# Three expert blocks joined on chip, the expert outputs read back ahead of the last weights, and the overflow loop moved into the middle of the stage

## The chip, the cores and the metric

One core of one Trainium2 chip. The metric is the device time of one execution in microseconds (us), taken as the median of the runs. Lower is better. PE is TensorE, DVE is VectorE, ACT is ScalarE, POOL is GpSimd and SP is SyncE; a "q" behind a name (SPq) is that engine's queue of transfers and waits.

## The reference, cut to what matters

Two layers. Each layer is a token mixer (gMLP in layer 0, RWKV-7 in layer 1) followed by a mixture of 32 experts; a final RMSNorm ends it. There are 768 tokens in layer 0 (512 latent and 256 context), and 512 in layer 1; a token is 1024 floats. All is float32. The part that the change touches is the experts' sum:

```python
def hier_moe(h, w_grp, b_grp, w_exp, b_exp, w_gate, w_up, w_down):   # h: n_tok x 1024
    ...                                   # router: two experts of 32 per token, with weights
    def expert_block(args):               # one block of up to 128 rows, one expert
        xb, e = args
        return (jax.nn.silu(xb @ w_gate[e]) * (xb @ w_up[e])) @ w_down[e]
    out = lax.map(expert_block, (buf.reshape(n_blocks, MOE_BLOCK, d), block_expert)).reshape(cap, d)
    y = jnp.zeros((n_assign, d), h.dtype).at[order].set(out[dest]).reshape(n_tok, TOP_K, d)
    return jnp.einsum('tk,tkd->td', weights, y)     # then x = x + gate * this
...
    return rmsnorm(x, final_g)                      # after the last layer, latent rows only
```

One expert has 1024x512 gate weights, as many up weights and 512x1024 down weights: 2 MB each, 6 MB in all. Every expert is used, so 192 MB of weights are read in each layer.

## The kernel before, in words

The experts are worked off in `Moe.experts`, in an order written once per layer (`self.seq`). A position of this order is one *unit*. A big unit (B) is one expert with up to 128 rows; a pair unit (p) is two experts with up to 64 rows each, which share the matrix engine by halves of its columns. Layer 0 has 12 p and 8 B, layer 1 has 13 p and 6 B. In the order of before, a p comes first, then B and p are mixed evenly, and a p is last. Positions are counted from 0: `gu(9)` below is the gate and up product of position 9.

A unit has these steps, in this order on PE: `gu` (L880: gate and up into the PSUM tile `gu_ps`, which needs the unit's gate and up weights), the hidden rows (ACT L943, DVE L944: `h_e`), their transposes (`eT_ps`, then `hT`), and `o` (L897: the down product into `o_ps`). The program places `o` of position i-1 after `gu` of position i. DVE scales `o_ps` to `yo` (L900), and POOL scatters `yo` by an indirect DMA (L809) into `ybuf`, a DRAM table with two rows per token. Rows of a unit's tokens come by a gather (`xg<-hbuf,idx`, POOL, L798).

The weights come in pieces of 1 MB, 12 pieces for a p, 6 for a B, issued by SP alone (`load`, L483, called by `fetch`). Pieces lie in the tiles `e_raw`: 13 buffers in layer 0, 15 in layer 1, handed out in rotation over three pools (`RAW = (2, 8, 3), (4, 6, 5)`: in layer 0 pieces go two to the first pool, eight to the second, three to the third, and again). A piece is issued when a buffer of its pool is free, which is when the product that read it is done, and when the eighth transfer before it has landed (SP's transfers have eight counters in turn). `want(i + 1)` makes the fetch of a unit stand one unit ahead of its `gu`; what SP does is in program order.

The last unit of a layer isn't scattered. Its `yo` is split in two parts (`y_parts`, L66 and L67) and each tile of 128 tokens takes its rows through a one-hot product (`c_ps`, L921) that DVE adds to the residual `x_res` (L924; `k.x` in the code). `early()` issues, when the last scatter is on its way, the reads of `ybuf` (L853: six pieces of 1 MB in layer 0, four in layer 1, into `e_raw`); POOL adds the two rows of each token (L856), DVE adds that to `x_res` (L916), for every third tile PE does it through the identity (L923). Then come, for each group of tiles, the squares (ACT L2093), a reciprocal root of few small instructions (L83 to L90), and in layer 0 the store of the tiles (`xd<-x_res`, SP), in layer 1 the final scaling (L2124, into `yo`) and the store of the output (L2125).

A unit may overflow in principle: `overflow` is a loop over a number `n_ov` that the chip works out. With this input it is zero and the loop's body never runs. It stands at the end of each layer's stage:

```python
        nv = nc.values_load(self.n_ov[:, 0:1], min_val=0, max_val=nmax)
        with tc.For_i(0, nv) as i:
```

The lines of the trace are those of the file before. The next stage after layer 0 begins with loads by SP (`a<-rw_a` L1313, `w_raw<-rw_wk` L1258), a memset by POOL (`hsel`, L1318), and DVE's scaling of `x_res` (L152).

Of the kernel before, what the change touches and what calls it, by code (L numbers as in the profile page):

```python
# [9 lines left out]
F32 = mybir.dt.float32  # L10
# [7 lines left out]
P = 128  # L18
# [305 lines left out]
class Moe:  # L324


    def __init__(self, k, l, n):
        self.k, self.l, self.n = k, l, n


        self.big = BIGS[l]
        self.pairs = (NE - self.big) // 2
        self.units = self.big + self.pairs

        self.nb = self.units + (2 * n * P) // 65
        rest, small = range(self.big), range(self.big, self.units - 1)
        self.seq = [self.units - 1] + [u for _, u in sorted(
            [((i + 0.5) / len(rest), u) for i, u in enumerate(rest)] + [((i + 0.6) / len(small), u) for i, u in enumerate(small)])]
        self.raw, self.slots = {}, 0
        self.scattered = []  # L340
# [14 lines left out]
    def open(self, ps, tag):  # L355
# [13 lines left out]
        self.tok = new([n], "tok")  # L369
# [132 lines left out]
    def route(self, rp, ps, after):  # L502
# [183 lines left out]
        u = self.seq[-1]  # L686
        for t in range(n):
            ts(self.tok[:, t:t + 1], tab[:, 1, u:u + 1], float(BIG - t * P), None, op0=ALU.add)
# [137 lines left out]
    def experts(self, ep, ps, after):  # L826
# [21 lines left out]
        def early():  # L848

            ys = []  # L850
            for t in range(n):
                y = self.slot().rearrange("p (k d) -> p k d", k=2)
                nc.sync.dma_start(y, self.ybuf[2 * t * P:2 * (t + 1) * P, :].rearrange("(p k) d -> p k d", k=2))  # L853
                ys.append(y)
            for y in ys:
                nc.gpsimd.tensor_tensor(y[:, 0, :], y[:, 0, :], y[:, 1, :], op=ALU.add)  # L856
            return ys

        xg, xT, hT = {}, {}, {}
# [4 lines left out]
        for i in range(N + 1):  # L864
# [5 lines left out]
            if i < N:  # L870
                want(i + 1)
                if i + XG - 1 < N:
                    xg[i + XG - 1] = self.gather(seq[i + XG - 1])
                q = {}
                for gu in range(2):
                    q[gu] = ps.tile([P, 512], F32, name="gu_ps", tag="gu", bufs=2)
                    for kk in range(KD):
                        f = slice(kk % 4 * 512, kk % 4 * 512 + 512)
                        for r, rows in self.ranks(seq[i]):
                            mm(q[gu][rows], xT[i][:, kk, rows], self.raw[r, 2 * gu + kk // 4][:, f], start=kk == 0, stop=kk == KD - 1)  # L880
                    if i + gu == 0:
                        xT[1] = transposed(xg[1], KD, "xT", 2)
                h = self.hidden(ep, q)
            if i + 2 < N:
                xT[i + 2] = transposed(xg[i + 2], KD, "xT", 2)
            if i == N - 2:
                one_hot = self.one_hot(ep)
            if i >= 1:
                u = seq[i - 1]
                g = self.gate(ep, self.ctx[:, u:u + 1])  # L890
                yo = ep.tile([P, D], F32, name="yo", bufs=YO)
                o = [ps.tile([P, 512], F32, name="o_ps", tag="eo", bufs=2) for _ in range(2)]
                for c in range(4):
                    for hf in range(2):
                        f = slice(c % 2 * 1024 + hf * 512, c % 2 * 1024 + hf * 512 + 512)
                        for r, rows in self.ranks(u):
                            mm(o[hf][rows], hT[i - 1][:, c, rows], self.raw[r, 4 + c // 2][:, f], start=c == 0, stop=c == 3)  # L897
                for hf in range(2):
                    f = slice(hf * 512, hf * 512 + 512)
                    stt(yo[:, f], o[hf], self.wslot[:, u:u + 1], g[:, f], op0=ALU.mult, op1=ALU.mult)  # L900
                if i < N:
                    self.scatter(u, yo)
                    if i == N - 1:
                        ys = early()
                else:
                    yh, yl = (ep.tile([P, D], F32R, name="y_parts", tag="xT", bufs=2) for _ in range(2))
                    for hf in range(2):
                        f = slice(hf * 512, hf * 512 + 512)
                        split(k, yh[:, f], yl[:, f], yo[:, f])
            if i < N:  # L910
                hT[i] = transposed(h, 4, "hT", 2)
        for g in after.groups:
            for t in g:
                by_pe = t % 3 == 2
                if not by_pe:
                    k.tc.keep_in_program_order(tt(k.x[:, t, :], k.x[:, t, :], ys[t][:, 0, :], op=ALU.add))  # L916
                for hf in range(2):
                    f = slice(hf * 512, hf * 512 + 512)
                    q = ps.tile([P, 512], F32, name="c_ps", tag=("gu", "eo")[t % 2], bufs=2)
                    for j, y in enumerate((yh, yl)):  # L920
# [98 lines left out]

RAW = (2, 8, 3), (4, 6, 5)  # L1020
H2 = (2, 4)
XG, YO = 4, 3


C = 64
# [1208 lines left out]
```

## Time and profile before

| | |
|---|---|
| time, median of 3 runs | 2669.89 us (2669.65 to 2680.07) |
| profiled execution: time, span | 2669.95 us, 2668.1 us |
| granted TensorE clock, mean | 0.934 of full speed |
| busy over the span | PE 89%, DVE 41%, ACT 28%, POOL 15% |
| moved by SP's queue (q1) | 608.69 MB |
| experts of layer 0, first gate product to the next stage | about 635 to 1175 us |
| experts of layer 1, first gate product to the end | about 2132 to 2668 us |

The span is the traced part of the execution; the time is 1.85 us longer than it. Busy shares are means over stages with different limits, and a busy PE is not PE at its peak, since the ends of matmuls are modelled. In the rows below "idle <- X" says what ended the idle time ahead of an instruction.

### The profile page before, as it was taken

The page shows a single profiled execution, that of the slowest core. Times are in us where ns is not written, and L with a number is a line of the kernel's source. Part 1 is how long each engine was busy: PE and PEld are TensorE (multiplying, and loading weights), DVE is VectorE, ACT ScalarE, POOL GpSimd, SP SyncE. Part 2 cuts the span into 40 slices and gives each one's busy share as a digit, 9 for nine tenths or more (in the row PEclk, how much of TensorE's full clock was granted, in tenths as well). Part 3 has the DMA queues.
Part 4 walks back from the last instruction along what each step waited for, and adds up shares of the span by engine and source line. Part 5 has one row for each costly group of instructions (what it writes and reads, how often), then busy time and mean ns, then how long its engine had stood idle before and what let it go on. Part 6 is the DMA issues. An engine that isn't in the chain of part 4 may idle for free. (4 is left out here: it accounts for less than half of the span.)

```text
span 2668.1 us, 38922 instructions
## 1 busy us (share of the span) xinstructions
PE 2369.2 (89%) x15466; PEld 1501.8 (56%) x15466; DVE 1095.0 (41%) x1976; ACT 743.1 (28%) x1256; POOL 400.6 (15%) x326
## 2 busy tenths in 40 slices
PE   5999999986999998968979999889888699999885
PEld 2778997763334433336745488778787433333331
DVE  4334334453122111177655274887787511111114
ACT  3222223331000000036654246566543200000001
POOL 0000000024332321230012012112212300000001
PEclk9999999997999999978978698999889799999997
DMA  7135317567999999942256464434236599999993
GB/s 247 56 126 198 103 64 233 185 234 286 390 420 419 419 410 416 384 150 84 72 179 176 140 180 120 96 92 105 69 107 204 213 364 419 419 417 411 419 415 157
DMA packets 280077, 640.23 MB, mean 240 GB/s; under 512 B 131084, under 2 KB 156940, under 8 KB 229460
## 3 DMA queue, kind: packets, MB, share of 16 engines
q1 hardware_dynamic: 266548, 608.69, 62.1%
q0 software_dynamic: 11904, 23.77, 2.4%
q10 hardware_dynamic: 1440, 5.24, 0.5%
q8 instruction: 123, 2.02, 0.3%
q14 instruction: 62, 0.51, 0.1%
HBM read 580.65 MB, written 76.02 MB: 246 GB/s over the span
## 5 line engine op out<-in xcount | busy, mean ns | idle before, releaser
L880 PE MATMUL gu_ps<-e_raw,xT 128*64 128x512 f32 (+1 forms) x2048 | 583.7, 601 | 25.7 <-DMA e_raw<-moe_w_up 16.8
L880 PEld LDWEIGHTS gu_ps<-e_raw,xT 128*64 128x64 f32 (+1 forms) x2048 | 206.6, 149 | 384.7 <-issue 311.5
L897 PE MATMUL o_ps<-e_raw,hT 128*64 128x512 f32 (+1 forms) x1024 | 299.8, 600 | 5.1 <-ACT hT L845 5.0
L944 DVE TENSOR_TENSOR h_e<-gu_ps,h_e 128x512 f32<-128x512 f32 x39 | 27.0, 691 | 503.5 <-PE gu_ps L880 503.5
L897 PEld LDWEIGHTS o_ps<-e_raw,hT 128*64 128x64 f32 (+1 forms) x1024 | 107.4, 148 | 159.0 <-issue 143.2
L943 ACT ACTIVATE h_e<-gu_ps 128x512 f32<-128x512 f32 x39 | 23.3, 597 | 589.0 <-PE gu_ps L880 589.0
L1114 PE MATMUL p<-ident 128*128 128x128 f32 x892 | 138.4, 298 | 8.3 <-ACT BKt L1799 4.3
L1114 PEld LDWEIGHTS p<-ident 128*128 128x128 f32 x892 | 116.5, 201 | 20.7 <-ACT BKt L1799 6.4
L809 POOL DMA_INDIRECT ybuf<-yo,idx x37 | 37.1, 1002 | 456.7 <-DVE yo L900 402.8
L900 DVE SCALAR_TENSOR_TENSOR yo<-o_ps,wslot,gt_e 128x512 f32<-128x512 f32 x40 | 29.9, 750 | 165.9 <-issue 113.5
L73 PE MATMUL u_ps<-hh,w_hi 128*128 128x384 f32 x256 | 90.7, 354 | 5.3 <-ACT w_hi L66 5.3
L845 ACT COPY xT<-eT_ps 128x512 f32<-128x512 f32 x39 | 22.8, 585 | 253.9 <-PE gu_ps L880 238.2
L798 POOL DMA_INDIRECT xg<-hbuf,idx x39 | 40.6, 1042 | 349.7 <-PE eT_ps L844 328.2
L900 DVE SCALAR_TENSOR_TENSOR yo<-o_ps,wslot,gt2B 128x512 f32<-128x512 f32 x38 | 28.4, 750 | 153.9 <-PE o_ps L897 152.5
L74 PE MATMUL u_ps<-hl,w_hi 128*128 128x384 f32 x256 | 87.7, 342 | 0.0
L75 PE MATMUL u_ps<-hh,w_lo 128*128 128x384 f32 x256 | 86.4, 342 | 1.2 <-DVE w_lo L67 1.2
L67 DVE TENSOR_TENSOR w_lo<-w_raw,w_hi 128x1024 fp32r<-128x1024 f32 x56 | 68.2, 1221 | 40.4 <-ACT w_hi L66 39.6
L123 PE MATMUL ada_ps<-w_raw,cstat 128*32 128x512 f32 x384 | 62.7, 615 | 21.2 <-DMA w_raw<-ada_w 20.9
L73 PE MATMUL v_ps<-w_hi,hh 128*128 128x512 f32 x192 | 75.4, 405 | 4.2 <-ACT w_hi L66 4.2
L66 ACT CAST w_hi<-w_raw 128x1024 fp32r<-128x1024 f32 x56 | 58.4, 1047 | 65.5 <-DMA w_raw<-ga_w_out 30.0
L74 PE MATMUL o_ps<-w_lo,gh 128*128 128x512 f32 x192 | 75.8, 396 | 0.0
L73 PE MATMUL o_ps<-w_hi,gh 128*128 128x512 f32 x192 | 75.5, 398 | 0.0
(555 smaller groups left out, 4484.0 us busy)
## 6 DMA issues: line engine op xcount, KB each, us to landing
e_raw<-moe_w_gate SPq DMA_DIRECT2D x128, 1024.0 KB
e_raw<-moe_w_up SPq DMA_DIRECT2D x128, 1024.0 KB
e_raw<-moe_w_down SPq DMA_DIRECT2D x128, 1024.0 KB
w_raw<-ada_w SPq DMA_DIRECT2D x96, 512.0 KB
w_raw<-ga_w_in SPq DMA_DIRECT2D x32, 512.0 KB
Td<-c_st SPq DMA_DIRECT2D x64, 192.0 KB
T<-Td SPq DMA_DIRECT2D x24, 512.0 KB
ybuf<-zero_rows SPq DMA_DIRECT2D x20, 512.0 KB
```

Of the source, the lines that this page charges most:

```text
L66: k.nc.scalar.copy(hi, src)
L67: k.nc.vector.tensor_tensor(lo, src, hi.bitcast(F32), op=ALU.subtract)
L73: mm(out, a[0], b[0], start=start, stop=False)
L74: mm(out, a[0], b[1], start=False, stop=False)
L75: mm(out, a[1], b[0], start=False, stop=stop)
L123: nc.tensor.matmul(q[32 * g:32 * g + 32, :], k.cstat[:, j, :], w, start=(j < 4), stop=(j >= 4), tile_position=(0, 32 * g))
L798: k.nc.gpsimd.indirect_dma_start(out=xg[:], out_offset=None, in_=self.hbuf[:, :], in_offset=bass.IndirectOffsetOnAxis(ap=self.idx[:, 1, b: ...
L809: st = self.k.nc.gpsimd.indirect_dma_start(out=self.ybuf[:, :], out_offset=bass.IndirectOffsetOnAxis(ap=self.idx[:, 0, b:b + 1], axis=0), ...
L880: mm(q[gu][rows], xT[i][:, kk, rows], self.raw[r, 2 * gu + kk // 4][:, f], start=kk == 0, stop=kk == KD - 1)
L897: mm(o[hf][rows], hT[i - 1][:, c, rows], self.raw[r, 4 + c // 2][:, f], start=c == 0, stop=c == 3)
L900: stt(yo[:, f], o[hf], self.wslot[:, u:u + 1], g[:, f], op0=ALU.mult, op1=ALU.mult)
L1114: nc.tensor.matmul(q[:, 0:128], self.ident, self.ident, start=True, stop=True)
```

## The change

- The last three positions (`HELD = 3`), all of them p, stay on chip: each is split and joined by one-hot products and DVE adds, so two scatters fewer in each layer. Positions N-3 and N-2 use a PSUM tile `c_ps` with one buffer.
- The reads of `ybuf` are issued ahead of the fetch of the last unit, no longer behind it. DVE adds both rows to the residual (L914, two instructions of 128x1024 for a tile); POOL's adds and PE's identity products are gone.
- The overflow loop moves from the end of the stage to the place ahead of position 9. The norm's groups no longer run in the loop.
- The order of units changes: the held p stand last, and the others are mixed in front. Layer 0 before: p p B p B p B p p B p B p B p p B p B p; now: p B p B p B p B p (loop) B p B p B p B p p p p. Layer 1 before: p p B p p B p p B p p B p p B p p B p; now: p p B p B p p B p (loop) B p p B p B p p p p.
- The norm of layer 0 has the groups of four and two tiles instead of three of two; the final scaling is done in place, and the output is stored from there. A root activation is written into the last unit.

```diff
-        rest, small = range(self.big), range(self.big, self.units - 1)
+        small, last = small[:len(small) - HELD], list(small[len(small) - HELD:])
...
             while state["loaded"] <= min(i, N - 1):
+                if state["loaded"] == N - 1:
+                    early()
                 self.fetch(state["loaded"])
...
-            for y in ys:
-                nc.gpsimd.tensor_tensor(y[:, 0, :], y[:, 0, :], y[:, 1, :], op=ALU.add)
...
+            if i < N - HELD:
+                self.scatter(u, yo)
+                return None
+            parts = [ep.tile([P, D], F32R, name="y_parts", tag="yo", bufs=YO) for _ in range(2)]
...
+        def add(one_hot, parts, t, last):
+            for hf in range(2):
+                tag, bufs = (("gu", 2), ("eo", 2))[t % 2] if last else ("c", 1)
+                q = ps.tile([P, 512], F32, name="c_ps", tag=tag, bufs=bufs)
+                for j, y in enumerate(parts):
+                    mm(q, one_hot[:, t * P:(t + 1) * P], y[:, half(hf)], start=(j == 0), stop=(j == 1))
+                tt(k.x[:, t, half(hf)], k.x[:, t, half(hf)], q, op=ALU.add)
...
+        behind = next(i for i in range(BEHIND + 3, N) if seq[i] < self.big)
+        for i in range(N):
+            if i == behind:
+                self.overflow(ep, ps)
...
+            if i == N - 1:
+                held = self.one_hot(HELD - 2), output(i - 1)
+                for t in range(n):
+                    for y in range(2):
+                        tt(k.x[:, t, :], k.x[:, t, :], ys[t][:, y, :], op=ALU.add)
+                    add(*held, t, False)
...
-        self.overflow(ep, ps, after)
...
-    groups = ((0, 1), (2, 3), (4, 5))
+    groups = ((0, 1, 2, 3), (4, 5))
```

**The loop in the stream of work.** PE's instructions in layer 0, after the change, from the fused end of position 8's gate product on (`eT_ps<-ident,h_e`: transposes of its hidden rows). Rows of L991 to L1026 are the loop's body, which isn't run.

```order
L922 MATMUL gu_ps<-e_raw,xT 64x512 x24
L847 MATMUL eT_ps<-ident,h_e 128x128 x4
L970 TENSOR_LOAD n_ov
L971 COMPARE_AND_BRANCH
L971 UNCONDITIONAL_BRANCH x2
...
L922 MATMUL gu_ps<-e_raw,xT 128x512 x16
L847 MATMUL eT_ps<-ident,xg 128x128 x8
L871 MATMUL o_ps<-e_raw,hT 64x512 x16
L847 MATMUL eT_ps<-ident,h_e 128x128 x4
L922 MATMUL gu_ps<-e_raw,xT 64x512 x32
L847 MATMUL eT_ps<-ident,xg 128x128 x8
L871 MATMUL o_ps<-e_raw,hT 128x512 x8
```

The loop stands between the transposes of position 8 and `gu(9)`; `o(8)` comes behind `gu(9)`, and `o(9)` behind `gu(10)`. SP's instructions at the same place, with what each waits for (DMAHW0 to DMAHW7 are the counters of SP's own transfers):

```order
L485 DMA e_raw<-moe_w_down 128x2048
L485 ISA
L485 DMA e_raw<-moe_w_down 128x2048
L970 TENSOR_LOAD n_ov
L971 COMPARE_AND_BRANCH
L971 UNCONDITIONAL_BRANCH [waits SP_sequencer_49,DMAHW0_49,DMAHW1_49,DMAHW2_49,DMAHW3_49,DMAHW4_49,DMAHW5_49,DMAHW6_49,DMAHW7_49]
...
L467 TENSOR_LOAD e_of
L467 ISA x2
L485 ISA
L485 DMA e_raw<-moe_w_gate 128x2048
```

SP has issued all pieces of position 9 there, waits for all of its transfers, and issues the first piece of position 10 behind the loop. PE, ACT and DVE wait on their branch for `barrier_Pool_Activation_PE_DVE_SP_release`. Before the change the same loop stood at the end (SP, layer 0):

```order
L853 DMA e_raw<-ybuf_61 128x2048 x6
L2098 DMA xd<-x_res 128x1024 x4
L952 TENSOR_LOAD n_ov
L952 ISA x2
L1258 DMA w_raw<-rw_wk 128x2x512
L953 COMPARE_AND_BRANCH
L953 UNCONDITIONAL_BRANCH x2
```

**The end of layer 0.** SP after the change: the six reads stand ahead of the last 12 pieces, and the next stage's loads follow the last piece with no loop between.

```order
L485 DMA e_raw<-moe_w_down 128x2048
L855 DMA e_raw<-ybuf_61 128x2048 x6
L467 TENSOR_LOAD e_of
...
L485 DMA e_raw<-moe_w_gate 128x2048
...
L485 DMA e_raw<-moe_w_down 128x2048
L1273 DMA w_raw<-rw_wk 128x2x512 x3
L2113 DMA xd<-x_res 128x1024 x4
```

PE after the change, from the end of position 18's gate product to the next stage:

```order
L847 MATMUL eT_ps<-ident,h_e 128x128 x4
L871 MATMUL o_ps<-e_raw,hT 64x512 x16
L888 MATMUL c_ps<-y_parts,xg 128x512 x20
L922 MATMUL gu_ps<-e_raw,xT 64x512
L888 MATMUL c_ps<-y_parts,xg 128x512 x4
L922 MATMUL gu_ps<-e_raw,xT 64x512 x31
L847 MATMUL eT_ps<-ident,h_e 128x128 x4
L871 MATMUL o_ps<-e_raw,hT 64x512 x16
L888 MATMUL c_ps<-y_parts,xg 128x512 x24
L158 MATMUL xT_l<-ident,x_res 128x128 x4
```

Twenty of the 24 one-hot products of position 18 stand ahead of the first product of `gu(19)`, the other four behind its first. DVE at that place (L889 is the add of a `c_ps`, L914 that of a read-back row, L962 the hidden rows of position 19):

```order
L914 TENSOR_TENSOR x_res<-x_res,e_raw 128x1024
L889 TENSOR_TENSOR x_res<-x_res,c_ps 128x512
L914 TENSOR_TENSOR x_res<-x_res,e_raw 128x1024
L889 TENSOR_TENSOR x_res<-x_res,c_ps 128x512 x3
L962 TENSOR_TENSOR h_e<-gu_ps,h_e 128x512
...
L889 TENSOR_TENSOR x_res<-x_res,c_ps 128x512 x12
L67 TENSOR_TENSOR w_lo<-w_raw,w_hi 128x1024
```

All 12 L914 and 12 L889 of position 18 stand ahead of position 19's L962; behind its `o` only its own 12 adds are left.

## Rows read from the trace of the kernel before

**Rows 1.** The middle of both expert stages (from, to, length in us; busy time and number of instructions of each engine; granted clock; mean busy share of the 16 DMA engines; GB/s).

```profile
640.00:1120.00 480.00, 455.13 (x1700) 185.72 (x1698) 73.93 (x151) 33.48 (x57) 135.98 (x73) 1.00 1.00 411
2180.00:2600.00 420.00, 385.75 (x1453) 153.46 (x1450) 55.30 (x124) 27.69 (x47) 26.11 (x26) 1.00 1.01 417
```

**Rows 2.** SP's waits in the expert stage of layer 0 (640 to 1130): line, what it waited for, us in total, times, longest.

```profile
SPq L483 <- DMA e_raw<-moe_w_gate: 111.6, 54, 3.2
SPq L483 <- PE gu_ps L880: 40.5, 24, 11.0
SPq L483 <- PE o_ps L897: 28.6, 10, 10.6
SPq L853 <- DMA ybuf<-yo,idx: 11.9, 1, 11.9
```

**Rows 3.** SP's issues at the end of layer 0's weights and of layer 1's: start, us from the first issue of the row to the end of its last, how many. Each issue lasts about 0.33 us.

```profile
1106.26 7.81 SPq L483 DMA_DIRECT2D e_raw<-moe_w_down  x4
1126.06 4.09 SPq L853 DMA_DIRECT2D e_raw<-ybuf  x6
...
2592.60 7.82 SPq L483 DMA_DIRECT2D e_raw<-moe_w_down  x4
```

**Rows 4.** The chain that ended last, in layer 1 (start, us, what): the flight of a piece from issue to landing, and one whole unit of PE.

```profile
2365.47 21.01 DMA e_raw<-moe_w_down
2408.03 3.66 PE gu_ps L880 x14
2411.78 0.70 DVE h_e L944
2412.53 1.62 PE eT_ps L844 x12
2414.15 7.58 PE o_ps L897 x32
2421.72 13.94 PE gu_ps L880 x32
2435.76 0.70 DVE h_e L944
```

**Rows 5.** The same chain at the start of layer 1's experts, where PE had waited: the first gate product, and the up product behind it; and a stretch there (columns as in rows 1).

```profile
2132.43 9.76 PE gu_ps L880 x32
2143.11 7.02 PE gu_ps L880 x32
...
2132.00:2137.00 5.00, 5.00 (x14) 1.52 (x15) 0.00 (x0) 0.00 (x0) 0.00 (x0) 0.50 1.03 420
```

**Rows 6.** The end of layer 0, in order of time: start, us, instruction [idle time before it <- what ended it].

```profile
1132.66 7.14 PE L897 MATMUL o_ps<-e_raw,hT 128*64 128x512 f32 x32 [0.73 <-ACT hT L845]
1137.42 16.96 POOL L856 TENSOR_TENSOR e_raw<-e_raw 128x1024 f32<-128x1024 f32 x6 [18.79 <-DMA e_raw<-ybuf]
1139.82 0.62 ACT L66 CAST y_parts<-yo 128x512 fp32r<-128x512 f32 x1 [7.21 <-DVE yo L900]
1140.51 5.04 DVE L67 TENSOR_TENSOR y_parts<-yo,y_parts 128x512 fp32r<-128x512 f32 x2
1168.94 1.06 ACT L2093 ACTIVATE e_raw<-x_res 128x1024 f32<-128x1024 f32 x1
1170.12 0.17 DVE L83 TENSOR_SCALAR r34v<-ssq 128x2 f32<-128x2 f32 x1 [1.26 <-ACT e_raw L2093]
1172.16 0.16 DVE L90 TENSOR_TENSOR rstd<-r34s,r34t 128x2 f32<-128x2 f32 x1
1175.09 0.75 DVE L152 TENSOR_SCALAR x_res<-x_res,rstd 128x1024 f32<-128x1024 f32 x1
```

**Rows 7.** Stretches of 2 us at the end of layer 0 (columns as in rows 1).

```profile
1122.00:1124.00 2.00, 2.00 (x12) 0.72 (x10) 0.00 (x0) 0.41 (x1) 0.00 (x0) 1.00 0.44 184
1148.00:1150.00 2.00, 0.31 (x1) 0.31 (x2) 1.90 (x3) 0.00 (x0) 2.00 (x1) 0.50 0.04 16
```

**Rows 8.** The adds on the residual at the end of layer 0 (times in ns: least, median, most); and DVE's share of a split of 128x1024, the same operation as `y_parts`' of 128x512, over the whole execution (busy us, mean ns of one, idle time before).

```profile
L924 DVE TENSOR_TENSOR x_res<-x_res,c_ps x12: 678/683/689, 1148.9 to 1168.2; 128x512 f32<-128x512 f32 x12
L916 DVE TENSOR_TENSOR x_res<-x_res,e_raw x4: 1226/1615/3375, 1145.5 to 1165.0; 128x1024 f32<-128x1024 f32 x4
...
L67 DVE TENSOR_TENSOR w_lo<-w_raw,w_hi 128x1024 fp32r<-128x1024 f32 x56 | 68.2, 1221 | 40.4 <-ACT w_hi L66 39.6
```

**Rows 9.** The chain at the end of layer 1.

```profile
2625.91 0.75 DVE yo L900
...
2638.60 2.07 PE c_ps L921 x4
2652.90 1.14 ACT e_raw L2093 x2
2655.45 1.28 DVE yo L2124
```

**Rows 10.** Around the loop at the end of layer 0 as it was: SP's issues, and the first conversions of what they loaded (512 KB each).

```profile
1173.30 0.35 SPq L1313 DMA_DIRECT2D a<-rw_a  x1
1173.70 1.32 SPq L1258 DMA_DIRECT2D w_raw<-rw_wk  x2
...
1173.43 0.20 POOL L1318 MEMSET hsel<- 128x128 f32 x1 [2.77 <-DVEq L953]
1178.78 1.05 ACT L66 CAST w_hi<-w_raw 128x1024 fp32r<-128x1024 f32 x1 [4.10 <-DMA w_raw<-rw_wk]
```

More of the change, by code (lines that the diff above doesn't have):

```diff
@@ L869, in experts @@
                     self.late_table(ep, ps, self.place_ov, self.block_ov, self.units, self.nb, part)
[L870 to L883, printed above, removed]
+            want(i + 1)
@@ new lines, in experts @@
+            if i + XG - 1 < N:
+                xg[i + XG - 1] = self.gather(seq[i + XG - 1])
+            if i == N - 1:
[4 more added lines that the diff above has]
+                    add(*held, t, False)
+            q = {}
+            for gu in range(2):
+                q[gu] = ps.tile([P, 512], F32, name="gu_ps", tag="gu", bufs=2)
+                for kk in range(KD):
+                    f = slice(kk % 4 * 512, kk % 4 * 512 + 512)
+                    for r, rows in self.ranks(seq[i]):
+                        mm(q[gu][rows], xT[i][:, kk, rows], self.raw[r, 2 * gu + kk // 4][:, f], start=kk == 0, stop=kk == KD - 1)
+                if i + gu == 0:
+                    xT[1] = transposed(xg[1], KD, "xT", 2)
@@ L884, in experts @@
+            h = self.hidden(ep, q)
             if i + 2 < N:
                 xT[i + 2] = transposed(xg[i + 2], KD, "xT", 2)
[L886 to L909, printed above, removed]
@@ L910, in experts @@
-            if i < N:
-                hT[i] = transposed(h, 4, "hT", 2)
+            if 1 <= i < N - 1:
+                parts = output(i - 1)
+                if parts:
+                    one_hot = self.one_hot(0)
+                    for t in range(n):
+                        add(one_hot, parts, t, False)
+            if i == N - 1:
+                one_hot = self.one_hot(HELD - 1)
+                nc.scalar.activation(self.sm.tile([P, 1], F32, name="root"), k.ones[:, 0:1], AF.Sqrt)
+            hT[i] = transposed(h, 4, "hT", 2)
@@ L912, in experts @@
+        parts = output(N - 1)
+        junk = self.xgp.tile([P, D], F32, name="xg", bufs=XG)
         for g in after.groups:
             for t in g:
[L914 to L920, printed above, removed]
-                        mm(q, one_hot[:, t * P:(t + 1) * P], y[:, f], start=(j == 0), stop=(j == 1 and not by_pe))
-                    if by_pe:
-                        nc.tensor.matmul(q, k.ident, ys[t][:, 0, f], start=False, stop=True)
-                    tt(k.x[:, t, f], k.x[:, t, f], q, op=ALU.add)
@@ L925, in experts, with one_hot @@
-                after.tile(t, ys[t][:, 1, :])
+                add(one_hot, parts, t, True)
+                after.tile(t, junk)
             after.group(g, ep)
-        self.overflow(ep, ps, after)
-    def one_hot(self, ep):
+    def one_hot(self, i):
         k = self.k
@@ L945, in hidden, with overflow @@
         return h
[L947 removed]
+    def overflow(self, ep, ps):
         k, l, n = self.k, self.l, self.n
```

51 lines of the change are left out of this document (30 added, 21 removed).

## The prediction

> **What bounds the kernel now.** I read the page's slices first, which say in which stretches the DMA engines are full, and then the stretches themselves. In the middle of both expert stages the 16 DMA engines are busy all the time, at 411 and 417 GB/s, while PE is busy for 95% and 92% [rows 1]. So the weights bound, with PE close behind in layer 0. SP's waits say the same: most of the time it waits for the eighth transfer before to land, in waits of up to 3.2 us, 111.6 us for gate pieces alone; it waits for PE's buffers for 69 us in layer 0 [rows 2]. SP issues a piece of 1 MB each (7.81 - 0.33)/3 = 2.49 us [rows 3], and a piece lands some 21.0 us after its issue [rows 4], about eight pieces later. A p thus takes 12 x 2.49 = 30 us of transfer, a B 15 us; PE takes 24.0 us for either (2411.8 to 2435.8) [rows 4].
>
> At the ends the picture turns. Layer 0's last piece is issued at 1113.7 and so lands at about 1134.8; the six reads come behind it, at 1126.1, because SP waits 11.9 us for the last scatter [rows 2, 3]. The half of the DMA engines that has run ahead stands idle meanwhile (0.44 busy), the other half is still at the weights [rows 7]; the reads land until 1134.8 + 6 x 2.49 = 1149.7, when the traffic has died out (0.04 busy) [rows 7]. PE ends its last `o` at 1139.8, and from there to the next stage's first scaling at 1175.1 it is 35.3 us [rows 6] of DVE, POOL and ACT. In layer 1 the last piece lands at 2600.1 + 21 = 2621.1, `o` ends at 2625.9, and the last scaling at 2656.7: 30.8 us [rows 3, 9].
>
> **The change, part by part.** The sum is made against the profiled execution, 2669.95 us, of which 2668.1 is the span; the median is 2669.89, so no correction is needed.
>
> *Reads ahead of the last weights.* The last piece of weights moves behind the reads: +6 x 2.49 = 14.9 us in layer 0, +4 x 2.49 = 10.0 in layer 1. Two scatters fewer in each layer: 512 KB each, an estimate of half a piece, 1.25 us, so -2.5 in each. `o` ends 5.0 us (layer 0) and 4.8 us (layer 1) behind the last landing, as now.
>
> *The tail behind `o`.* Now 35.3 us in layer 0. POOL's six adds take 17 us there and slow DVE while they run: L67 takes 2.5 us for each half of `y_parts`, where the mean of 128x1024 is 1.22 and a half thus about 0.7, and L916 takes 3.38, against 1.23 when POOL is done [rows 6, 8]. After: the second half's scaling 0.75, the two parts 0.62 and 0.7, the first product 0.5, then 12 adds of 0.683 us = 8.2 [rows 6, 8, 9], the last square with its read-out 1.25, the root 2.2 (1170.12 to 1172.32) [rows 6], and some 0.2 for a split of the next stage's weights that stands between: 14.5. That saves 20.8 us. Layer 1 likewise: 2.6 + 8 x 0.683 = 5.5, square 1.25, root 1.4 (2654.04 to 2655.45), four scalings of 1.28 [rows 9], and up to 0.7 for the load of a root table: 16.5, which saves 14.3. The stores of the output end as now, behind the last scaling. The adds moved from POOL to DVE lie in the last unit, beside `gu`: nothing, with one exception below.
>
> Without loop and order: layer 0, 14.9 - 2.5 - 20.8 = **-8.4**; layer 1, 10.0 - 2.5 - 14.3 = **-6.8**; together -15.2.
>
> *The loop.* It costs nothing by its body, but it makes SP wait until all its transfers have landed, and the others wait for each other. At the end of the stage, where it was, hardly anything was in flight. In the middle there is: when `gu(8)` ends, 3.7 us after its last up piece landed, its four down pieces and the six of position 9 are still to come, 25 us. PE is through with the transposes after 6 us [rows 4], so it stands for 19 us, and 1 us more for the loop (the last root ended at 1172.3, SP issued again at 1173.3) [rows 6, 10]. Then the queue is empty. The row nearest to a restart: 512 KB and a second 512 KB, issued from 1173.30 on, have landed when ACT starts at 1178.78, 5.5 us later [rows 10]; a full queue delivers 1 MB in 2.49. So the least is 1.0 + 5.5 - 2.5 = 4.0 us a layer.
>
> More is lost because SP has no lead any more. Of layer 0's 13 buffers 10 still hold pieces of positions 8 and 9. The pool of three holds both down pieces of position 9, until `o(9)`, which comes behind `gu(10)`; the 13th piece after the loop, the first of position 11, takes its place in that pool. Counted from the barrier: `gu(9)` 14.0, hidden rows and transposes 2.3, `o(8)` 7.6, `gu(10)` 14.0, 2.3, half of `o(9)` 3.8 = 44.0, and 2.7 more for the half clock after the wait (9.76 against 7.02 us, granted clock 0.50 against 1.00: 1.2 and 2.4 GHz) [rows 4, 5]; plus about 5 for a landing from rest [rows 10]: 49 to 52 us. Without a loop that piece lands after 13 x 2.7 = 35 (2.7 is a piece with its share of gathers and scatters, an estimate: 2.49 x 1.09). That loses 14 to 17 us; I take 16. In layer 1, with 15 buffers, the sixth piece waits for `o(8)`: 14.0 + 2.3 + 3.8 = 20.1, up to 22.8, plus 1.0 and 5, against 6 x 2.7 = 16.2: 10 to 12; I take 11. The upper bound is PE's whole stand, 20 + 2.7 us a layer, if nothing of it is made up; the lower 4.0.
>
> The price of a transfer from rest is also stated by the Trainium skill, "DMA: Bandwidth & Descriptors", section on the anatomy of one DMA: about 2.0 us fixed plus bytes at 436 GB/s. By it the least would be 1.0 + 2.0 = 3.0 us a layer, and the whole sum 2 us lower, if that path's price holds for SP's queue.
>
> *The order of units.* In layer 0 a B now stands second, when buffers are short: SP waits for PE there, at most 10.6 and 11.0 us at once [rows 2]. I take +3, between 0 and 7 (part of one such wait).
>
> *Products of position 18 ahead of `gu(19)`.* Each tile takes two L914 of 1.23, two adds of 0.68 and a pair of products, 1.0, that waits for the only `c_ps`: about 4.9 us, 29 us for six [rows 8, 9]. The weights of position 19 need 15 + 20 us behind those of 18. So PE starts late but is about ready when the last piece lands: +1, between 0 and 7; layer 1's four tiles, 20 us, are covered.
>
> Sum: -15.2 + 16 + 11 + 3 + 1 = +15.8, hence 2669.95 + 15.8 = **2686 us**.
>
> **The rivals.** A, the forecast: the loop costs what the buffers say; 2677 to 2697.
> B, the loop costs only the restart. For it: the eight-buffer pool hands out what is free first, and PE, with 24 us a unit against a mean of 24 of transfer in layer 0 and 25 in layer 1, may make up a wait at the B units. Then -15.2 + 2 x 4.0 + 3 = -4: 2666.
> C, the other side: the drain hides. SP waits 69 us for PE's buffers in layer 0 [rows 2]; if PE, not the queue, is what the stream waits for around position 9, the drain falls into such a wait, and what is left is the shorter tail: -15.2 + about 0, 2655. It decides when both loops together, order included, cost under 2 us. Against it: the DMA engines are full from 640 to 1120 [rows 1].
> D, the last unit on top: in layer 0 PE can't start `gu(19)` until DVE is through, and the stand at the loop is lost whole: -15.2 + 2 x 20 + 3 + 7: 2705. Against it: PE has 25 us of slack in layer 0 and 34 in layer 1 [rows 1].
> E, a fetch of code: each engine jumps over the loop's body. Where the loop was, POOL's next work came 2.8 us after DVE's queue, and SP's after 1.0 [rows 10], so 1.8 us a layer could come on top of A: 2690. The Trainium skill, "Runtime: NRT & Kernel Launch", section on instruction fetch, says that a taken branch to code outside the window makes the engine fetch it. No row here prices it in the middle of a stream.
>
> **How the numbers follow.** A 0.50, B 0.20, C 0.12, D 0.13, E 0.05. The time is A's, 2686. The range leaves out most of C's and the far part of D: 2660 to 2702. What can be told from no change is 0.5%, 13.3 us: faster is under 2656.6, slower above 2683.2. Faster comes from C, with 0.01 for a gain at the next stage's start that I did not price: 0.13. Slower comes from D, E and three quarters of A: 0.55. The same comes from B and the rest of A: 0.32.
>
> **What would show it.** In each layer one stretch of some 20 us about the middle of the stage where PE is idle, with SP waiting at the loop's lines, the DMA share falling to about half and then nought for some us; after it, a second dip of the share some 30 to 40 us later in layer 0, with SP waiting for `o` (the line L871), and one about 15 us later in layer 1. If there is no second dip, B is right. The stage's last piece should land 31 us later than now in layer 0 (14.9 - 2.5 + 16 + 3) and 18 later in layer 1, and from the end of `o` it should be 14.5 us to the next stage's L152 and 16.5 to the last scaling, with no POOL add. DVE's L914 should take 1.23 us. I am wrong if PE's stand is under 10 us, if the tails shrink by less than 25 us together, or if the wait for DVE ahead of `gu(19)` sets the end of layer 0.

## The result and the profile after

The changed kernel takes 2696.96 us (median of five runs, 2694.91 to 2701.59) against 2669.65 us for the kernel before, run beside it. The ratio is 1.0106 (95% interval 1.0077 to 1.0135, written in brackets from here on): 27 us slower. The forecast was 2686, with a range of 2660 to 2702.

The profiled execution took 2701.59 us (span 2699.3, 31.2 more than before). The additional time by stretches, from the rows below and those of before:

| stretch | before | after | difference |
|---|---|---|---|
| start of the program to the next stage's first scaling (L152) | 1175.09 [rows 6] | 1202.93 | +27.8 |
| from there to layer 1's first gate product | 957.3 [rows 5, 6] | 954.2 | -3.1 |
| from there to the last scaling | 523.0 [rows 9] | 537.0 | +14.0 |
| from there to the end of the span | 12.6 | 5.1 | -7.5 |

The page of after: the DMA engines' share and GB/s in the 40 slices, and two groups of PE. Its columns are as in the page's section 5: busy, mean ns, idle time before and what ended most of it.

```profile
DMA  7136226566998999941245564434236599989994
GB/s 244 60 121 214 83 78 234 195 229 264 417 421 346 375 421 419 406 157 54 94 157 168 146 184 118 103 88 108 72 96 199 210 378 421 421 321 421 421 421 190
...
L922 PE MATMUL gu_ps<-e_raw,xT 128*64 128x512 f32 (+1 forms) x2048 | 603.5, 610 | 23.6 <-SPq L971 20.3
...
L888 PE MATMUL c_ps<-y_parts,xg 128*128 128x512 f32 x120 | 51.2, 529 | 35.8 <-DVE x_res L889 27.6
```

The two slices at 346 and 321 GB/s hold the loop, one in each layer; PE stands 20.3 us there in both together. PE's one-hot products were preceded by 35.8 us of standing, most of it for DVE's adds into the residual. That is the larger sum, and the forecast had 1 us for it.

SP's waits in layer 0 (640 to 1130), as in [rows 2]:

```profile
SPq L485 <- PE o_ps L871: 109.6, 30, 14.2
SPq L485 <- PE gu_ps L922: 109.5, 44, 14.2
SPq L485 <- DMA e_raw<-moe_w_gate: 57.9, 31, 3.2
```

SP now waits 219 us for PE's buffers, where it was 69 [rows 2], and half as long for landings of gate pieces (57.9 us, where it was 111.6). The stretch between loop and position 18 has PE busy for 209.72 of 214 us (columns as in rows 1):

```profile
866.00:1080.00 214.00, 209.72 (x770) 83.81 (x771) 24.03 (x34) 14.75 (x25) 71.66 (x38) 1.00 0.99 404
```

All of the standing in this stretch is for other engines: 4.3 us for DVE's hidden rows, none for weights. The kernel before was already near this. Its PE stood for, in layer 0 (640 to 1130):

```profile
PE eT_ps L844 <- DVE h_e L944: 16.4, 16, 3.5
PE gu_ps L880 <- DMA e_raw<-moe_w_up: 3.9, 3, 1.4
PE gu_ps L880 <- DMA e_raw<-moe_w_gate: 2.4, 2, 1.7
```

Only 6.3 us of PE's idle time there was a wait for weights; most went to DVE's hidden rows, which every unit needs. So in layer 0 the changed kernel hangs on PE, not on the weights, and what holds PE up moves the end.

**The loop.** PE there in layer 0 and in layer 1 (start, us, instruction, idle time before and what ended it):

```profile
854.91 0.66 PE L847 MATMUL eT_ps<-ident,h_e 128*128 128x128 f32 x4 [0.86 <-DVE h_e L962]
862.62 15.39 PE L922 MATMUL gu_ps<-e_raw,xT 128*128 128x512 f32 x32 [7.05 <-SPq L971]
...
2391.85 17.07 PE L922 MATMUL gu_ps<-e_raw,xT 128*128 128x512 f32 x32 [13.24 <-SPq L971]
```

Stretches of layer 0 behind it, columns as in rows 1:

```profile
862.00:866.00 4.00, 3.38 (x5) 1.59 (x6) 0.00 (x0) 0.00 (x0) 3.48 (x2) 0.57 0.15 20
...
872.00:884.00 12.00, 12.00 (x47) 5.21 (x47) 1.39 (x2) 0.59 (x1) 5.41 (x4) 1.00 1.01 419
...
892.00:906.00 14.00, 14.00 (x59) 5.75 (x56) 1.39 (x2) 1.18 (x2) 2.54 (x2) 1.00 0.69 280
```

The queue runs empty (0.15 busy), fills again, and dips a second time some 30 us later (0.69), as forecast. PE's stand is 7.05 us in layer 0 and 13.24 in layer 1, not 20.

**The end of layer 0.** In the kernel before, the gate product of position 18 there:

```profile
1091.97 14.00 PE L880 MATMUL gu_ps<-e_raw,xT 128*128 128x512 f32 x32
```

PE after, and below it DVE (same columns):

```profile
1090.12 1.02 PE L922 MATMUL gu_ps<-e_raw,xT 128*64 128x512 f32 x2
...
1097.98 1.19 PE L888 MATMUL c_ps<-y_parts,xg 128*128 128x512 f32 x2 [3.67 <-DVE x_res L889]
...
1125.85 0.73 PE L888 MATMUL c_ps<-y_parts,xg 128*128 128x512 f32 x2
...
1128.16 7.14 PE L871 MATMUL o_ps<-e_raw,hT 128*64 128x512 f32 x32 [0.73 <-ACT hT L848]
1136.05 0.50 PE L888 MATMUL c_ps<-y_parts,xg 128*128 128x512 f32 x1 [0.75 <-ACT y_parts L66]
...
1155.38 1.22 PE L888 MATMUL c_ps<-y_parts,xg 128*128 128x512 f32 x2 [0.78 <-DVE x_res L889]
...
1163.58 15.05 PE L922 MATMUL gu_ps<-e_raw,xT 128*64 128x512 f32 x62
...
1180.81 7.14 PE L871 MATMUL o_ps<-e_raw,hT 128*64 128x512 f32 x32 [0.68 <-ACT hT L848]
...
1155.24 1.22 DVE L914 TENSOR_TENSOR x_res<-x_res,e_raw 128x1024 f32<-128x1024 f32 x1
1156.64 0.69 DVE L889 TENSOR_TENSOR x_res<-x_res,c_ps 128x512 f32<-128x512 f32 x1 [0.18 <-PE c_ps L888]
...
1190.17 7.38 DVE L889 TENSOR_TENSOR x_res<-x_res,c_ps 128x512 f32<-128x512 f32 x12
...
1202.93 0.75 DVE L152 TENSOR_SCALAR x_res<-x_res,rstd 128x1024 f32<-128x1024 f32 x1
```

Stretches of 2 us at the end of either layer's weights (columns as in rows 1):

```profile
1160.00:1162.00 2.00, 1.65 (x3) 0.50 (x2) 0.31 (x1) 0.00 (x0) 0.00 (x0) 0.50 0.01 4
...
2662.00:2664.00 2.00, 2.00 (x12) 0.62 (x10) 0.00 (x0) 0.60 (x1) 0.00 (x0) 1.00 0.00 0
```

Read it as one chain. `gu(18)` begins at 1090.12, 1.9 us earlier than in the kernel before, in spite of the loop. With position 17's products threaded through it, it ends at 1126.6: 36.5 us in place of 14.0. Then come position 18's products: a pair takes 1.22 us at a granted clock of 0.50 (0.73 at 1.00), and only when the add of 0.69 has read it may the next pair write the only `c_ps`: one half tile every 2.00 us, PE standing 0.78 of it. From the first at 1136.05 to the rest of `gu(19)` at 1163.58 it is 27.5 us. The weights have all landed by about 1161 (0.01 busy), so PE and not the queue is late: `o` ends at 1187.95, some 27 us behind the landing, where it was 5.0. From there to L152 it is 15.0 us.

**The end of layer 1**: PE's first gate product of the layer and its last two steps, the last scaling, and SP's stores of the output.

```profile
2157.14 9.74 PE L922 MATMUL gu_ps<-e_raw,xT 128*64 128x512 f32 x32
...
2654.93 15.19 PE L922 MATMUL gu_ps<-e_raw,xT 128*64 128x512 f32 x62
...
2672.30 7.14 PE L871 MATMUL o_ps<-e_raw,hT 128*64 128x512 f32 x32 [0.67 <-ACT hT L848]
...
2694.18 1.28 DVE L2138 SCALAR_TENSOR_TENSOR x_res<-x_res,rstd,fgB 128x1024 f32<-128x1024 f32 x1
...
2690.52 5.31 SPq L2139 DMA_DIRECT2D out_dram<-x_res  x4
```

The weights have landed by 2662 (0.00 busy behind it); `o` ends at 2679.4, 17 us later, where it was 4.8. From there to the end of the last scaling it is 16.0. From that to the end of the span it is 3.8 us, where it was 11.4 (2668.1 - 2656.7).

### The profile page after: what moved, and what is told of

Its sections match the earlier page's. It is cut to its first block, busy times and chain, and to the rows that moved or that the text cites. A ratio compares the mean times of both kernels' runs of the same rounds, so it can differ in the third digit from the quotient of the medians.

```text
span 2699.3 us, 39036 instructions
## 1 busy us (share of the span) xinstructions
PE 2412.3 (89%) x15534; PEld 1514.6 (56%) x15534; DVE 1136.9 (42%) x2049; ACT 747.8 (28%) x1265; POOL 368.0 (14%) x312
## 5 line engine op out<-in xcount | busy, mean ns | idle before, releaser
L922 PE MATMUL gu_ps<-e_raw,xT 128*64 128x512 f32 (+1 forms) x2048 | 603.5, 610 | 23.6 <-SPq L971 20.3
L962 DVE TENSOR_TENSOR h_e<-gu_ps,h_e 128x512 f32<-128x512 f32 x39 | 27.0, 692 | 465.4 <-PE gu_ps L922 412.2
L1129 PE MATMUL p<-ident 128*128 128x128 f32 x892 | 143.8, 306 | 9.0 <-ACT BKt L1814 4.5
L888 PE MATMUL c_ps<-y_parts,xg 128*128 128x512 f32 x120 | 51.2, 529 | 35.8 <-DVE x_res L889 27.6
L1844 DVE TENSOR_TENSOR X<-X,subt 128x31 f32<-128x31 f32 (+15 forms) x186 | 73.7, 396 | 5.0
L75 PE MATMUL v_ps<-w_hi,hl 128*128 128x512 f32 x192 | 75.7, 394 | 0.0
```

What stands on the lines that cost most here:

```text
L75: mm(out, a[1], b[0], start=False, stop=stop)
L888: mm(q, one_hot[:, t * P:(t + 1) * P], y[:, half(hf)], start=(j == 0), stop=(j == 1))
L1129: nc.tensor.matmul(q[:, 0:128], self.ident, self.ident, start=True, stop=True)
L1844: eng.tensor_tensor(x, x, t.t.rearrange("p (a b) -> p a b", a=31 - j), op=ALU.subtract)
```

## The experiments

Each ran beside the kernel before on the same chip; the ratios are to it, and differences in us between kernels are ratios times 2667. The lines of each trace are those of that kernel's own file, so the same product has another line number in some of them.

### e1: no loop at all

```diff
-            if i == behind:
-                self.overflow(ep, ps)
```

The overflow loop is left out of the program; with this input its body never runs.

> The changed kernel with the overflow loop left out (with this input its body never runs). Theory: the loop stops the stream of weights once a layer, 14 us in layer 0 and 13 us in layer 1 counted at pieces of the same number, and what follows only comes later by that; the wait of the last gate product for the held blocks' adds is a cost of its own. Then this kernel takes 2697 - 27 = 2670 us, and in layer 0 o(19) still ends over 20 us behind the landing of the last piece. Rival: the late matrix engine at the end of each layer is what was lost at the loop and never made up. Then 22 and 11 us more come back: about 2637 us, and o(19) ends about 5 us behind the last landing.

Measured 2674.41 us, ratio 1.0027 [1.0010, 1.0045]. The loop in the middle costs 0.79%, 21 us for both layers, against 27 in the forecast; the two intervals together leave it some 9 us either way. The profiles put it at 19.5: L152 comes at 1195.86, 7.1 us earlier, and layer 1 takes 524.6 us from its first gate product to its last scaling, 12.4 less than 537.0. The rest of the change was forecast to gain 11 us (-15.2 + 3 + 1); it loses 7. So a part of the loss is not the loop's. Nor does PE's lateness come from the loop, as the rival had it:

```profile
1156.17 15.37 PE L920 MATMUL gu_ps<-e_raw,xT 128*64 128x512 f32 x62
...
1173.73 7.14 PE L871 MATMUL o_ps<-e_raw,hT 128*64 128x512 f32 x32 [0.68 <-ACT hT L848]
```

Without a loop the products of position 18 still take 27.5 us (1128.63 to 1156.17), and `o` still ends at 1180.9, some 25 us behind the last traffic (0.08 busy from 1154, 0.00 from 1156).

### e2: the loop behind the last gate product

```diff
-            if i == behind:
-                self.overflow(ep, ps)
...
+        self.overflow(ep, ps)
+        one_hot = self.one_hot(HELD - 1)
```

> The changed kernel with the loop moved from position 9 to the place behind the last unit's gate product, ahead of its down product, where the last pieces are landing anyway. Theory: as without a loop, plus about 1 to 3 us a layer for a barrier that finds nearly nothing in flight: 2672 to 2676 us. Rival (a loop costs the same wherever it stands): no gain, 2697 us.

Measured 2673.90 us, ratio 1.0028 [1.0012, 1.0044], the same as with no loop. PE stands 2.29 us there in layer 0, behind transfers that have landed anyway (0.00 busy from 1158 to 1172), and `o` behind it takes 8.78 us in place of 7.14:

```profile
1173.87 8.78 PE L871 MATMUL o_ps<-e_raw,hT 128*64 128x512 f32 x32 [2.29 <-issue]
```

So the loop costs what is in flight at its place, and not much by itself. The Trainium skill, "Runtime: NRT & Kernel Launch", section on instruction fetch, has a taken branch out of the window wait for code; e1 and e2 lie 0.5 us apart for two loops, with intervals of over 4 us each way, so no run here shows a price of it.

### e3: the kernel before, its loop in the middle

```diff
+        behind = next(i for i in range(BEHIND + 3, N) if seq[i] < self.big)
...
+            if i == behind:
+                self.overflow(ep, ps)
...
-        self.overflow(ep, ps, after)
```

> The kernel before with nothing changed but the loop's place: ahead of a big unit in the middle (the first from position 9 on), and without the norm's groups in its body. Theory: +14 and +13 us in the two stages, and about 7.5 us less at the end of the program, where the loop stood behind the last store: 2670 + 20 = 2690 us. Rival (the late matrix engine at the end comes from the loop): +27 + 33 - 7.5, about 2722 us. If the loop is hidden by buffers: 2662 us.

Measured 2679.01 us, ratio 1.0044 [1.0026, 1.0061]: 12 us slower, not 20. PE at the loop in layer 0, SP's last four pieces of either layer, L152, and the last scaling:

```profile
878.36 16.27 PE L883 MATMUL gu_ps<-e_raw,xT 128*128 128x512 f32 x32 [19.77 <-SPq L955]
...
1123.80 7.81 SPq L483 DMA_DIRECT2D e_raw<-moe_w_down  x4
...
1186.67 0.75 DVE L152 TENSOR_SCALAR x_res<-x_res,rstd 128x1024 f32<-128x1024 f32 x1
...
2615.67 7.82 SPq L483 DMA_DIRECT2D e_raw<-moe_w_down  x4
...
2677.54 1.28 DVE L2122 SCALAR_TENSOR_TENSOR yo<-x_res,rstd,fgB 128x1024 f32<-128x1024 f32 x1
```

Where the weights bound, the loop does what the forecast said: a stand of 19.77 us, and last pieces 17.5 us later in layer 0 (1106.26 before) and 11.5 in layer 1 (23.1 at 2592.60, less 11.6 from layer 0) [rows 3]. Forecast were 16 and 11. But it gives back what it had cost at its old place: L152 comes 11.6 us later, so 5.9 returned in layer 0, and from the end of the last scaling to the end of the span (2682.6) it is 3.8 us in place of 11.4, so 7.6 returned at the end of the program. The forecast had said of those stores that they end as now.

### e4: the adds and products in another order

```diff
             if i == N - 1:
                 held = self.one_hot(HELD - 2), output(i - 1)
                 for t in range(n):
-                    for y in range(2):
-                        tt(k.x[:, t, :], k.x[:, t, :], ys[t][:, y, :], op=ALU.add)
                     add(*held, t, False)
+                for t in range(n):
+                    for y in range(2):
+                        k.tc.keep_in_program_order(tt(k.x[:, t, :], k.x[:, t, :], ys[t][:, y, :], op=ALU.add))
...
-                if parts:
-                    one_hot = self.one_hot(0)
-                    for t in range(n):
-                        add(one_hot, parts, t, False)
...
+            if 1 <= i < N - 1 and parts:
+                one_hot = self.one_hot(0)
+                for t in range(n):
+                    add(one_hot, parts, t, False, True)
```

The `True` at the end pins the first product of each pair in the written order, behind `gu(18)`. The loop stays in the middle.

> The changed kernel, loop at position 9 as it is, with another order of the held adds: the products of position N-3 are pinned behind the gate product of position N-2, and VectorE's adds of the returned rows come behind the adds of position N-2, no longer between them. Theory: the last gate product starts 10 to 14 us sooner in layer 0 and 5 to 11 in layer 1: 2697 - 20 = 2677 us, loop cost unchanged. Rival (the late matrix engine comes from the loop): 2697 us.

Measured 2687.73 us, ratio 1.0066 [1.0033, 1.0099]: 11 us of the 20 expected, and since this interval overlaps that of the changed kernel, the size is loose. The chain is still there, and `gu(19)` comes 4.8 us earlier only:

```profile
1144.93 1.22 PE L888 MATMUL c_ps<-y_parts,xg 128*128 128x512 f32 x2 [0.78 <-DVE x_res L891]
...
1158.82 13.95 PE L925 MATMUL gu_ps<-e_raw,xT 128*64 128x512 f32 x62
```

The L914 fitted into the gaps of DVE: without them a half tile still takes 2.00 us. Position 17's products were moved, not removed: they now lie between those of `o(18)`, which takes 16.1 us (1112.90 to 1129.03) in place of 7.14.

### e5 and e6: two buffers for the products

```diff
-                tag, bufs = (("gu", 2), ("eo", 2))[t % 2] if last else ("c", 1)
+                tag, bufs = (("gu", 2), ("eo", 2))[t % 2] if last else ("eo", 2)
...
                 for t in range(n):
-                    for y in range(2):
-                        tt(k.x[:, t, :], k.x[:, t, :], ys[t][:, y, :], op=ALU.add)
                     add(*held, t, False)
+                for t in range(n):
+                    for y in range(2):
+                        k.tc.keep_in_program_order(tt(k.x[:, t, :], k.x[:, t, :], ys[t][:, y, :], op=ALU.add))
```

e5 is this with the loop in the middle, e6 with the loop behind the last gate product, as in e2.

> The changed kernel, loop at position 9 as it is, with the held blocks' products in the two PSUM tiles of the down product (tag eo, 2 buffers) instead of one tile of their own, and the adds of the returned rows behind position N-2's adds. Theory: what keeps the last gate product back is a chain of one product pair and one add at a time through a single PSUM tile, with 1.22 us adds in between; with two tiles and the long adds out of the way the pairs follow each other in 0.7 to 0.8 us. The stand of 22 us in layer 0 and 11 us in layer 1 goes: 2697 - 30 = 2667 us (2660 to 2675), the loop's cost unchanged. Rival (the products' mere place ahead of the gate product costs it, whatever the tiles): as the run with the reordered adds, 2688 us.

> The same with the loop behind the last unit's gate product. Theory: the loop's 22 us come off on top: 2645 us, faster than the kernel before by 0.8%. Rival (what the loop's place gave there is hidden once the end is not late any more): 2665 us.

Measured: e5 2666.00 us, ratio 0.9981 [0.9960, 1.0003]; e6 2649.64 us, ratio 0.9922 [0.9897, 0.9947]. PE and DVE at the end of layer 0 of e6:

```profile
1118.40 8.82 PE L888 MATMUL c_ps<-y_parts,xg 128*128 128x512 f32 x23 [0.23 <-DVE y_parts L67]
...
1140.51 3.65 PE L920 MATMUL gu_ps<-e_raw,xT 128*64 128x512 f32 x14 [1.30 <-DMA e_raw<-moe_w_up]
...
1151.20 9.07 PE L871 MATMUL o_ps<-e_raw,hT 128*64 128x512 f32 x32 [5.53 <-SPq L969]
...
1127.86 14.45 DVE L913 TENSOR_TENSOR x_res<-x_res,e_raw 128x1024 f32<-128x1024 f32 x12
...
1175.23 0.75 DVE L152 TENSOR_SCALAR x_res<-x_res,rstd 128x1024 f32<-128x1024 f32 x1
```

23 products take 8.82 us, 0.77 a pair, in place of 2.00; the twelve adds of read-back rows run beside `gu(19)`; and `gu(19)` waits for its weights again, so the weights bound the end once more. Both theories held: e5 lies 33 us below the changed kernel, and the loop's place is worth 16 us between e5 and e6, by the ratios. e6 beats the kernel before by 21 us and the changed one by 49.

Two things remain in e6. The loop is not free there: the weights are only just landing, so PE stands 5.53 us for it (5.61 in layer 1), and `o` behind it takes 9.07 us (9.80) in place of 7.14; what e6 would take with no loop, no run shows. And the changed end of the stage gains nothing in layer 0: L152 comes at 1175.23, where it was 1175.09. Of the 17.8 us by which e6's span is shorter, 7.8 lie behind the last scaling, where the loop had stood, 3 in layer 1 and 7.1 between the layers (see "The middle" below).

The Trainium skill, "Perfetto Trace Analysis", section on matmuls, says that independent groups of products should rotate through several PSUM banks, so that one group's read-out runs beside the next one's products. The trace agrees: 2.00 us a half tile with one, 0.77 with two.

### e7: the read-back behind the last weights

```diff
             while state["loaded"] <= min(i, N - 1):
-                if state["loaded"] == N - 1:
-                    early()
                 self.fetch(state["loaded"])
                 state["loaded"] += 1
+                if state["loaded"] == N:
+                    early()
...
+        for t in range(n):
+            add(one_hot, parts, t, True)
+            for y in range(2):
+                tt(k.x[:, t, :], k.x[:, t, :], ys[t][:, y, :], op=ALU.add)
+        self.overflow(ep, ps)
```

With two buffers, as in e6, but the reads behind the last weights as before the change, their adds beside position 19's, and the loop behind all adds.

> Three blocks held, two PSUM tiles, and the reads of the table issued behind the last weights again as in the kernel before; VectorE adds both rows of a tile as they land, beside the last down product; the loop behind all adds and ahead of the norm. Theory: reads ahead of the last weights put 15 and 10 us of transfer ahead of the last down product and its adds, about 15 us of tail that nothing overlaps; reads behind them land while that tail runs. Against the run with the loop behind the last gate product: 10 to 15 us less in each layer, about 2622 us (2615 to 2640). Rival (the change's order is right, since the long adds on the returned rows then lie behind the last landing): 2645 us or more.

Measured 2670.68 us, ratio 1.0003 [0.9988, 1.0019]: 22 us slower than e6, where 2622 us had been expected; the rival held. SP's reads, the last of DVE's adds, and L152:

```profile
1125.54 19.85 SPq L855 DMA_DIRECT2D e_raw<-ybuf  x6
...
1178.39 3.61 DVE L938 TENSOR_TENSOR x_res<-x_res,e_raw 128x1024 f32<-128x1024 f32 x3
...
1190.80 0.75 DVE L152 TENSOR_SCALAR x_res<-x_res,rstd 128x1024 f32<-128x1024 f32 x1
```

The 14.5 us of adds then lie behind the last `o`, and the whole norm behind them. The loop's place differs between e6 and e7 too, and no run separates the two; the profiles do in part. In layer 0 `o` ends 1.6 us earlier than in e6 (1158.6 against 1160.3), but the last add on the residual ends 23.4 us behind it in place of 9.6, ahead of the loop: 13.8 us for the adds. From there to L152 it is 8.8 us in place of 5.4: 3.4, which may be the loop's. In layer 1 the two kernels lie 1 us apart (521.1 and 520.0 us from the first gate product to the last scaling). So reading ahead of the last weights was worth its place in layer 0; in layer 1 it made no difference that these profiles show.

### e8 and e9: the buffers alone, the order alone

e8 is e2 with the one line of e5 that names the buffers; e9 is e2 with the order of e4.

> The loop stands behind the last gate product (where it cost nothing measurable), and only the held tiles' buffer is changed: c_ps of positions N-3 and N-2 takes the two buffers of the tile o_ps has, the read-back rows' adds stay between the tiles' products as in the changed kernel. Theory 'both the one buffer and the order hold PE': with two buffers PE's products still wait for DVE, which has two L914 of 1.22 us and two adds of 0.69 us for each tile, 3.8 us a tile or 23 us for six in layer 0 against some 27 us for the chain before; PE gains 4 to 6 us in layer 0 and less in layer 1, so 2666 to 2671 us. Rival 'the one buffer alone is it': products run ahead, gu(19) waits for weights, 2650 to 2655 us.

> The same place of the loop, and only the order is changed: the products and adds of position N-3 are pinned behind the gate product of N-2, and the read-back rows' adds come behind all products of N-2; c_ps keeps its one buffer. Theory 'both hold PE': 24 products in pairs of 2.0 us, of which an add takes 0.69, still 20 us or more ahead of gu(19); some 9 us less than the 2674 us of the kernel that only moves the loop, as with the loop in the middle: 2663 to 2667 us. Rival 'the order alone is it': 2650 to 2655 us.

Measured: e8 2659.92 us, ratio 0.9973 [0.9958, 0.9987]; e9 2668.20 us, ratio 1.0013 [1.0000, 1.0025]. With the loop at the same place in all four:

| | one buffer | two buffers |
|---|---|---|
| adds between the products | 1.0028 (e2) | 0.9973 (e8) |
| adds behind the products | 1.0013 (e9) | 0.9922 (e6) |

The buffers alone give 15 us. The order alone gives 4, which is within the intervals (11 in e4, whose interval is wider). Both give 28, so with the buffers there the order is worth 14 more. e8 fell between its two theories, which had looked at position 18 alone. In layer 0 of e8 (PE):

```profile
1080.01 1.02 PE L919 MATMUL gu_ps<-e_raw,xT 128*64 128x512 f32 x2
...
1099.87 7.08 PE L919 MATMUL gu_ps<-e_raw,xT 128*64 128x512 f32 x30
...
1117.08 0.50 PE L888 MATMUL c_ps<-y_parts,xg 128*128 128x512 f32 x1 [0.75 <-ACT y_parts L66]
...
1133.12 2.08 PE L888 MATMUL c_ps<-y_parts,xg 128*128 128x512 f32 x4 [1.39 <-DVE x_res L889]
...
1140.30 13.95 PE L919 MATMUL gu_ps<-e_raw,xT 128*64 128x512 f32 x62
```

Position 18's products still take 23.2 us, 3.47 a tile, since DVE has two L914 and two L889 for each: the first theory's price. But `gu(18)` with position 17's products takes 26.9 us (1080.0 to 1106.9) instead of 36.5, and that neither theory had.

## Why the forecast was right, and where it was not

The direction, the range and most of the mechanisms held. The size came from one large error and several small ones against it, and that the time lies inside the range is partly luck, as the sum below shows.

**The step that failed: "Products of position 18 ahead of `gu(19)`", +1 us, layer 1's "covered".** The chain's price was nearly right: 29 us were forecast for six tiles, 27.5 measured. Wrong was that PE had slack for it. "PE starts late but is about ready when the last piece lands" took the landing as what PE waits for; in layer 0 PE stood for no weight between the loop and position 18 (209.72 of 214 us busy), so nothing covered the chain. The 25 us of slack that the forecast held against rival D were PE's idle time in the kernel before, and only 6.3 us of it was a wait for weights. `o` ended 27 us behind the landing instead of 5, so the term was 22 in layer 0, and 12 in layer 1 (17 instead of 4.8). Position 17's products, which no term had, added 22 us to `gu(18)` in layer 0 and are part of the same delay. e5, e6 and e8 show the cause: with two buffers the delay falls by half, with two buffers and the other order it is gone, and e1 shows that it does not come from the loop. This is rival D's place, with a wait of PE for DVE ahead of `gu(19)`; the time was not D's, since the stand at the loop was small. The sign that was named for being wrong, that this wait sets the end of layer 0, is there.

**The loop, +16 and +11.** The mechanism is right: drain, stand, second dip, and e3 has 17.5 and 11.5 on the kernel before. In the changed kernel it cost 21 us and not 27 (e1), by the profiles 7.1 in layer 0, where 16 had been forecast, and 12.4 in layer 1, where it was 11, with a stand of 7.05 and 13.24 us instead of 20. In layer 0 less was in flight when the loop came: from the end of SP's last issue to PE's next product it is 11.7 us (851.0 to 862.6), in e3 21.0 (857.4 to 878.4). The traffic had dipped shortly before (0.44 busy from 840 to 844), and in the 51 us up to that last issue SP had waited 29.3 us for PE's buffers, in e3 16.2. By the mark set ("under 10 us") layer 0's stand is a miss. In layer 0 PE lost 7.05 us and 1.4 more in the product behind it (15.39 us against 13.95 for a `gu` elsewhere), 8.5 in all.

**What the loop cost at its old place.** "The stores of the output end as now" was wrong: 7.6 us came back at the end of the program, in after as in e3. For layer 0 the new tail, built up from its instructions, already held that gain.

**The tails.** 14.5 forecast and 15.0 measured in layer 0; 16.5 and 16.0 to the end of the last scaling (14.7 to its start) in layer 1. L914 took 1.22 us (1.23 forecast), the adds of a tile's halves 0.62 in a row (7.38 us for twelve). They shrank by 20.3 and 14.8 us, as forecast.

**The reads and the last piece.** Layer 0's weights landed by about 1161, 26 us later than 1134.8, where 31 had been forecast. In layer 1 they landed 505 us behind its first gate product (2662 - 2157.1), 16 us more than before (2621.1 - 2132.4), where 18 had been forecast. So the reads' 14.9 and 10.0 us are borne out in the sum with the loop, not by themselves. Nor can the +3 for the order of units be told from it: SP's waits for PE, 219 us instead of 69, may come from that order or from what PE carries besides, which no run separated.

**The middle.** Between the layers 3.1 us were saved that no step had. This stretch took 957.3 and 957.7 us in the two kernels with the old end of the stage (before and e3), and 944.6 to 954.8 in the nine with the new one, though its own code is the same in all. No run separated the cause, and a difference of a few us between two profiles says little there.

The sum, remade: 15.8 + 21 + 12 (PE late) - 5 - 2 (last pieces) - 7.5 (end of the program) - 3.1 = 31, against 31.2 of the profiled execution. With the first error alone the forecast would have been 33 us too low, the kernel at some 2719 us and outside the range; the others hid half of that.

The rivals: B (restart only, 8 us for both loops) and C (drain hides, under 2) fall with e1, which puts 21 us on the loop, though C's condition, a stream that waits for PE's buffers around position 9, is what layer 0 shows. E is not settled: its 1.8 us a layer are too little for e1 and e2 to tell. What a transfer from rest costs, on which the forecast weighed the Trainium skill's "DMA: Bandwidth & Descriptors", no run isolated, since PE waited for no weight behind the loop in layer 0.

## What to carry to other kernels

Before work is put ahead of the last unit of a stream, look whether the engine that takes it really waits for the stream there: a landing that comes just ahead of the engine's end says nothing of slack, the "idle before" column does. A product that goes through one PSUM buffer and an add costs the sum of both for each tile; give it two, and put other adds of the same engine behind the whole group. A loop that makes all queues drain belongs where nothing is in flight any more but work still goes on: behind the last gate product it cost nothing measurable in e2, whose transfers had landed (in e6, whose last weights were still landing, PE stood 5.5 us for it), in the middle 21 us, and at the very end 7.6.

## What the hardware showed that was not expected

PE's granted clock was 0.50 (1.2 of 2.4 GHz) in the chain, in which PE stood for 0.78 of every 2.00 us, so a pair of products took 1.22 us instead of 0.73: 6 us over twelve pairs, beside the standing itself. The 62 products of `gu(19)` behind it took 15.05 us, of which the first began at 0.50 (0.54 from 1164 to 1166, 1.00 from 1166 on). In e6, where the products came without such a stand, they were at 1.00 from the start: 23 in 8.82 us.
